# A five-branch mixer: the state-space projections as seven-product jobs, and branch d behind the jobs

## The chip, the cores and the metric

The kernel runs on 1 core of a Trainium2 chip. The metric is the device time of one execution in microseconds (us). A core has five engines that run their own instruction streams in order: TensorE (PE, matmuls), VectorE (DVE), ScalarE (ACT), GpSimd (POOL) and SyncE (SP, which here issues most DMAs). They wait for each other by semaphores.

## What is computed

One layer of a mixer over L = 1024 tokens and 1024 channels: one input projection feeds five branches, each is projected to 1024 channels, and the five are merged by sigmoid gates. The parts of the reference that matter here are branch d and the merge:

```python
def causal_depthwise_conv(x, w, b=None):
    ...
    y = xp[:, 0:L] * w[0]
    for j in range(1, K):            # K = 4
        y = y + xp[:, j:j + L] * w[j]
    return y if b is None else y + b

def ssd_branch(z, xbc, dt_in, conv_w, conv_b, a_log, dt_bias, d_skip, norm_g):
    xbc = jax.nn.silu(causal_depthwise_conv(xbc, conv_w, conv_b))
    xs, bm, cm = split(xbc)          # 512, 2 x 128, 2 x 128 channels
    dt = softplus(dt_in + dt_bias); cs = cumsum(dt * a)      # per chunk of 128 tokens
    xdt = xs * dt
    lmat = where(incl, exp(cs[t] - cs[s]), 0)
    cb = einsum('bncgd,bnsgd->bngcs', cm, bm)
    y_diag = einsum('bngcs,bngrcs,bnsgrp->bncgrp', cb, lmat, xdt)
    states = einsum('bnsgd,bngrs,bnsgrp->bngrpd', bm, decay_states, xdt)
    ...                              # scan over the chunks gives s_prev
    y = y_diag + y_off + xs * d_skip
    return rms_norm(y * silu(z), norm_g)

for p in range(5):
    merged = merged + sigmoid(h @ w_gate[p]) * (ys[p] @ w_branch[p])
x = x + merged @ w_out
```

## The kernel before

**Products.** Every fp32 operand is split into a high and a low part, and a 128x512 product is three matmuls per 128 of K (high by high, high by low, low by high). A *direct* projection of a block of 128 channels over 1024 tokens (`proj_in`, tile `gin`) is 8 K-steps x 2 halves x 3 = 48 matmuls. A gate block (`gate_half`, tile `gate`) is as many.

**Seven-product jobs.** `seven` computes two blocks of 128 channels at once, as a 2x2 block product with seven instead of eight half products: 7 x 12 = 84 matmuls (tile `pm`) instead of 96. The sums of weights it needs (`factors`: `fs`) are made on POOL, their split on ACT (`fh`) and DVE (`fl`), and seven DVE steps (`u`, `c`, `x`) put the products together. The sums of the token operand, which all jobs share, are made once before the first job, in the pool `ct`: 16 POOL sums `r`, DVE sums and splits (`fs`, `s`, `t1l`, `t2l`, `t4l`), at last `h01l`. The products lie in eight PSUM banks (`open_banks("pt", x=8)`, handed out in turn). The results go to DRAM and a branch fetches them with `loaded`.

**Stages**, with their times in the trace: a prologue with the token index scores of branch c (to 175 us); branch a (to 555.6); branch d with its twelve direct blocks, and four gate blocks between its steps (`marks`, `gate_mm`), then `ct`, with c's block `c_k` and the last gate block (to 816.6); 30 jobs, 14 for projections of b, m and c and 16 for gates (to 1390.5); branch b and branch m (to 1559.5); branch c; the output projection. A merge multiplies one branch's result by `w_branch` (16 half blocks of 12 matmuls, tile `proj`, 192 in all), and adds it under its gate. The order of merges is `seq` = (0, 3, 1, 4, 2): branch a, d, b, m, c. Merge 0 is put beside branch b and merge 1 beside m, by `issue_after`: a half block may be issued after a given matmul of the branch, these marks lying `evenly` in it.

**Branch d** works in two groups of four heads. A group takes four blocks (two of `x`, one each of B and C), each a `conv_silu`: three shifted DVE products over 1023, 1022 and 1021 columns, a Tanh and a closing product. Eight units follow, one for 128 tokens, two of them in flight (`skew`): `lm` loaded by a DMA, four DVE steps (subtract, min), Exp on ACT, four DVE products with `dt` and the masked `cb`; then `pyd`, `pyo` and the state `dst`, with four POOL steps (`xw`, `xs`, `ytd`, `dst`). At the end, four blocks `zs` of z and eight gates (`yz`, `yf`).

**Top-k.** The selection of branch c is 192 pairs of DVE steps (MAX8 and MATCH_REPLACE8). `share` tells which part of them is put between the DVE work of branch a, branch d and the stage t (`ct` and the jobs).

Of the kernel before, what the change touches and what calls it, by code (L numbers as in the profile page):

```python
# [55 lines left out]
def mixer_body(ctx, tc, a, out):  # L56
# [1075 lines left out]
    def gate_mm(p, cb, mark, w):
        for hv in HV:
            with tc.issue_after(mark):
                run(gate_half(p, cb, hv, w))

    fill = []
    for (p, cb), mark in zip(units[len(done):], marks):
        fill.append((p, cb, mark, gate_w(p, cb)))
        if len(fill) < len(marks):  # L1140
# [271 lines left out]
```

## Time and profile before

| | us |
|---|---|
| median of 3 runs | 1928.08 (1925.49 to 1933.24) |
| the profiled execution | 1928.29 |
| its span | 1926.6 |
| PE busy | 1819.6 (94%) |
| DVE busy | 1535.1 (80%) |
| ACT busy | 765.1 (40%) |
| POOL busy | 546.0 (28%) |

The span is the time from the first to the last instruction that the hardware profiler recorded. A busy time counts an engine's instructions, overlaps once. The granted clock of PE is 1.0 at its full level, 2.4 GHz, and 0.5 at the lower one, 1.2 GHz. Idle time of an engine is shown before a row in square brackets with what ended it.

### The profile page before, as it was taken

How to read it: one execution, taken by the hardware profiler on the slowest of the kernel's cores; microseconds unless marked ns; L12 is line 12 of the kernel's file. 1: busy time of each engine (PE TensorE's matmuls, PEld its weight loads, DVE VectorE, ACT ScalarE, POOL GpSimd, SP SyncE). 2: the span in 40 equal slices, each digit the busy share in tenths (PEclk: the TensorE clock that was granted, in tenths of full speed). 3: DMA queues.
4: the chain of work that ended last, by engine and by line, in shares of the span. 5: the costliest groups of instructions: out<-in, count | busy, mean ns of one | idle time of the engine just before them, and what ended most of it. 6: DMA issues, size and time to landing. Idle time of an engine off the chain costs nothing.

```text
span 1926.6 us, 30311 instructions
## 1 busy us (share of the span) xinstructions
PE 1819.6 (94%) x11116; PEld 1490.7 (77%) x11116; DVE 1535.1 (80%) x2684; ACT 765.1 (40%) x1455; POOL 546.0 (28%) x518
## 2 busy tenths in 40 slices
PE   6999999999999999699999999999988989999888
PEld 5788787878788777588888888888766668887767
DVE  7679979788757997987787878777777669997874
ACT  6466242424234413333222234333334546764231
POOL 5102212121102232432222222222024254434144
PEclk9999999999999999899999999999999999999999
DMA  6412111111122222133333333332478353224533
GB/s 195 122 50 55 51 39 51 40 45 50 46 72 55 66 50 83 67 120 115 104 115 112 107 115 108 117 110 99 142 234 277 111 170 116 89 88 155 166 114 129
DMA packets 187909, 199.88 MB, mean 104 GB/s; under 512 B 23641, under 2 KB 139214, under 8 KB 187762
## 3 DMA queue, kind: packets, MB, share of 16 engines
q1 hardware_dynamic: 187186, 196.91, 32.5%
q8 instruction: 88, 1.44, 0.3%
q10 hardware_dynamic: 576, 1.05, 0.1%
q14 instruction: 59, 0.48, 0.1%
HBM read 141.67 MB, written 52.05 MB: 101 GB/s over the span
## 4 chain that ended last, share of the span: by engine, by line
PE 71%; DVE 16%; issue 4%; DMA 3%; ACT 3%; POOL 2%; SPq 0%; POOLq 0%; DVEq 0%; ACTq 0%
PE pm L50 31%; PE gin L50 13%; PE proj L50 8%; PE po L50 3%; PE lg L50 2%; PE gate L50 2%; DVE sc L50 2%; PE pT L50 2%; PE ix L50 2%; DVE m L50 1%; DVE cacc L50 1%; PE t L50 1%; PE t2y L50 1%; DVE wlo L50 1%; DVE lm L50 1%
## 5 line engine op out<-in xcount | busy, mean ns | idle before, releaser
L50 PE MATMUL proj<-part,whi 128*128 128x512 f32 x640 | 209.4, 402 | 7.8 <-DVE tgl L50 2.8
L50 DVE MAX8 m<-sc 128x8 f32<-128x384 f32 (+5 forms) x192 | 170.3, 888 | 1.6
L50 DVE MATCH_REPLACE8 sc<-m,sc 128x384 f32<-128x384 f32 (+5 forms) x192 | 168.0, 875 | 0.0
L105 ACT ACTIVATE fh<-fs 128x512 fp32r<-128x512 f32 x132 | 83.1, 632 | 193.7 <-PE pm L50 188.0
L50 PEld LDWEIGHTS proj<-part,whi 128*128 128x128 f32 x640 | 120.6, 191 | 34.4 <-DVE tgl L50 4.0
L50 PE MATMUL proj<-part,wlo 128*128 128x512 f32 x320 | 128.2, 401 | 4.8 <-DVE wlo L50 4.8
L105 ACT ACTIVATE whi<-wraw 128x512 fp32r<-128x512 f32 x106 | 66.3, 629 | 144.0 <-PE gin L50 94.3
L50 DVE SCALAR_TENSOR_TENSOR u<-pm,u 128x512 f32<-128x512 f32 x128 | 85.0, 684 | 47.5 <-PE pm L50 47.2
L105 ACT ACTIVATE fh<-gr 128x512 fp32r<-128x512 f32 x90 | 56.8, 632 | 145.6 <-PE pm L50 113.5
L50 DVE TENSOR_TENSOR fl<-fs,fh 128x512 fp32r<-128x512 f32 x132 | 93.8, 713 | 3.5 <-ACT fh L105 3.5
L1187 POOL TENSOR_TENSOR fs<-gr 128x512 f32<-128x512 f32 x30 | 39.0, 1301 | 184.3 <-DVE fl L50 183.5
L1333 POOL TENSOR_TENSOR mg<-mg,tgl 128x512 f32<-128x512 f32 x48 | 67.8, 1416 | 57.2 <-DVE tgl L50 52.5
L50 DVE TENSOR_TENSOR fl<-gr,fh 128x512 fp32r<-128x512 f32 x90 | 64.1, 713 | 24.5 <-ACT fh L105 24.5
L50 DVE SCALAR_TENSOR_TENSOR cacc<-craw,pc,cacc 128x1023 f32<-128x1023 f32 (+2 forms) x60 | 77.6, 1293 | 3.6 <-ACT cacc L543 3.2
L50 DVE TENSOR_TENSOR wlo<-wraw,whi 128x512 fp32r<-128x512 f32 x82 | 60.2, 738 | 18.7 <-ACT whi L105 13.7
L50 PEld LDWEIGHTS proj<-part,wlo 128*128 128x128 f32 x320 | 60.8, 190 | 16.8 <-DVE wlo L50 5.2
L1186 POOL TENSOR_TENSOR fs<-gr 128x512 f32<-128x512 f32 x30 | 39.4, 1315 | 116.8 <-issue 116.8
L910 ACT ACTIVATE lg<-lg,mx,rq 128x128 f32<-128x128 f32 (+7 forms) x64 | 55.0, 861 | 18.7 <-DVE mx L50 16.4
L50 DVE SCALAR_TENSOR_TENSOR lg<-sc,cf,lg 128x384 f32<-128x384 f32 (+3 forms) x96 | 56.2, 604 | 6.8 <-POOL cf L889 3.8
L50 PE MATMUL pm<-h00h,fl 128*128 128x512 f32 x120 | 47.8, 398 | 12.6 <-DVE fl L50 12.6
L50 DVE SCALAR_TENSOR_TENSOR sc<-rl,iwt,sc 128x512 f32<-128x512 f32 (+3 forms) x84 | 47.0, 615 | 12.2 <-ACT rl L463 11.0
L922 ACT ACTIVATE pt<-pT 128x512 f32<-128x512 f32 (+3 forms) x96 | 43.1, 484 | 34.1 <-PE po L50 25.9
(601 smaller groups left out, 5628.1 us busy)
## 6 DMA issues: line engine op xcount, KB each, us to landing
tgl<-gd SPq DMA_DIRECT2D x80, 256.0 KB, 2.8
wraw<-in_w_in_dram SPq DMA_DIRECT2D x66, 256.0 KB, 2.8
gr<-in_w_gate_dram SPq DMA_DIRECT2D x32, 512.0 KB, 3.6
gr<-in_w_in_dram SPq DMA_DIRECT2D x28, 512.0 KB, 3.7
yr<-yd SPq DMA_DIRECT2D x40, 256.0 KB, 4.0
wraw<-in_w_branch_dram SPq DMA_DIRECT2D x40, 256.0 KB, 3.5
yd<-sg SPq DMA_DIRECT2D x16, 512.0 KB, 3.4
gd<-u SPq DMA_DIRECT2D x30, 256.0 KB, 4.0
```

The costliest lines, as they stand in the source:

```text
L50: r = f(*args, **kw)
L105: S.activation(hi, raw, AF.Copy)
L910: S.activation(lg[:, :W], lg[:, :W], AF.Exp, scale=rq[:, 2 * j + hf:2 * j + hf + 1], bias=mx[:, hf:hf + 1], accum_out=sm[:, hf:hf + 1])
L922: S.activation(pt[:, i0 * P:(i0 + n) * P], ps[:, :n * P], AF.Copy)
L1186: eng.tensor_tensor(s3, a11, a21, OP.subtract)
L1187: eng.tensor_tensor(s1, a21, a22, OP.add)
L1333: (G if n < 4 else V).tensor_tensor(m, m, t, OP.add)
```

## The change

- The eight blocks of `d_xbc` and the four of `d_z` are no longer direct blocks of branch d. They become six seven-product jobs: four for `d_xbc`, in the fifth to eighth place of the list, and two for `d_z` behind `c_gate`.
- The four jobs of `d_xbc` have the convolution as an epilogue, `conv_halves`: it works on the halves of 512 tokens as they leave `seven`, with its sums in PSUM banks from the same eight (`cacc`, two for each block), and small extra products where the second half needs the last tokens of the first.
- Branch d comes behind all jobs and loads its blocks. Merge 0 is now beside it; merge 1 is beside b and m together.
- The four gate blocks that stood between the steps of d are now made one after the other behind `c_k`.
- `share` gives branch a 0.25 and the stage t 0.75 of the top-k steps, d none.
- In a unit of d the four subtract-and-min steps become four ACT Relu, `dt` is put on `xs` instead of `lm` (a POOL product `xd` more; `xw` is made from it), and the four products with `cbm` become one DVE product of 512 columns.

```diff
@@ z blocks through DRAM
+          (..., ("d_z", 4), ("d_xbc", 8))}
@@ branch_d
-                tl.append(conv_silu(gp, proj_in(OFF["d_xbc"] + blk * P), [scw[:, j, blk:blk + 1] for j in range(4)],
-                                    ssdb[:, blk:blk + 1], "dc", "dc", 4))
+                tl.append(loaded(gp, "d_xbc", blk, "dc", 6))
...
                 for r in range(4):
-                    V.tensor_scalar(lm[:, r, :], lm[:, r, :], cs[:, n, 8 + 4 * g + r:9 + 4 * g + r], 0.0, OP.subtract, OP.min)
-                S.activation(flat(lm), flat(lm), AF.Exp)
-                for r in range(4):
-                    V.scalar_tensor_tensor(lm[:, r, :], lm[:, r, :], dtt[:, n, 4 * g + r:4 * g + r + 1], cbm, OP.mult, OP.mult)
+                    S.activation(lm[:, r, :], lm[:, r, :], AF.Relu, scale=-1.0, bias=cs[:, n, 8 + 4 * g + r:9 + 4 * g + r])
+                S.activation(flat(lm), flat(lm), AF.Exp, scale=-1.0)
+                V.tensor_tensor(lm, lm, cbm[:, None, :].to_broadcast([P, 4, P]), OP.mult)
                 xsn = v4(xs[:, n, :])
+                xd = gp.tile([P, 4, 64], F32, name="xd", tag="xd", bufs=2)
                 xw = gp.tile([P, 4, 64], F32, name="xw", tag="xw", bufs=2)
-                G.tensor_tensor(xw, xsn, b3(dte[:, n, hs], 4, 64), OP.mult)
+                G.tensor_tensor(xd, xsn, b3(dtt[:, n, hs], 4, 64), OP.mult)
+                G.tensor_tensor(xw, xd, b3(eds[:, n, hs], 4, 64), OP.mult)
...
-        zs = [silu2(gp, proj_in(OFF["d_z"] + b * P), "zs", "dc", 4) for b in range(4)]
+        zs = [silu2(gp, halves(loaded(gp, "d_z", b, "zr", 1)), "zs", "dc", 6) for b in range(4)]
...
-    share = {"a": 0.3, "d": 0.1, "t": 0.6}
+    share = {"a": 0.25, "t": 0.75}
...
     branch("a", branch_a)
-    branch("d", branch_d)
...
-        gate_mm(*fill[-1])
+        for _ in gate_steps(4):
+            pass
...
+    def conv_halves(c, cw, cb):
+
+        acc = [bank("cacc") for _ in c]
+        for y, x in zip(acc, c):
+            S.activation(y, x, AF.Identity, scale=cw[3], bias=cb)
+        for j in (2, 1, 0):
+            d = 3 - j
+            for y, x in zip(acc, c):
+                V.scalar_tensor_tensor(y[:, d:], x[:, :512 - d], cw[j], y[:, d:], OP.mult, OP.add)
+            V.scalar_tensor_tensor(acc[1][:, :d], c[0][:, 512 - d:], cw[j], acc[1][:, :d], OP.mult, OP.add)
+        for y, x in zip(acc, c):
+            S.activation(x, y, AF.Tanh)
+            V.scalar_tensor_tensor(x, x, 1.0, y, OP.add, OP.mult)
...
+            cs4 = seven(ga, w, mov)
+            if f == "conv":
+                for i in range(2):
+                    conv_halves(cs4[2 * i:2 * i + 2], [scw[:, j, b + i:b + i + 1] for j in range(4)], ssdb[:, b + i:b + i + 1])
...
     next(first)
+    branch("d", branch_d)
+    m0 += evenly(span["d"], 16)
+    run(first)
+    m0 = []
+    first = merge_steps(1, m0)
+    next(first)
...
     branch("b", branch_b)
-    m0 += evenly(span["b"], 16)
-    run(first)
     branch("m", branch_m)
     kmx.close()
-    merge(1, [None] * 4 + evenly(span["m"], 12))
+    m0 += evenly(span["b"] + span["m"], 16)
+    run(first)
```

Three places in the order of instructions. On DVE, where the sums of the job operands begin, before (`flo` is the low part of a gate block's weights, `fs`, `s`, `r`, `t1l`, `t2l`, `t4l` are the sums, `yz`, `yf` the gates of branch d):

```order
L50 TENSOR_SCALAR dss<-dss 128x1
L50 TENSOR_TENSOR yf<-pyT,pc 128x512
L50 TENSOR_SCALAR yz<-yz,dss 128x512
L50 MATCH_REPLACE sc_128<-m_68,sc_128 128x768
L50 TENSOR_TENSOR yf<-pyT,pc 128x512
L50 TENSOR_TENSOR flo<-fraw,fhi 128x512
L50 TENSOR_TENSOR fs<-r_7526,r_7528 128x512
L50 TENSOR_TENSOR flo<-fraw,fhi 128x512
L50 TENSOR_TENSOR s_7524<-r_7530,r_7526 128x512
L50 TENSOR_TENSOR fs<-r_7530,fs 128x512
L50 TENSOR_TENSOR t1l<-fs,t1h 128x512
L50 TENSOR_TENSOR r_7532<-fs,r_7532 128x512
```

The end of the same sums after the change:

```order
L50 TENSOR_TENSOR t4l<-r_5726,t4h 128x512
L50 TENSOR_TENSOR s_5679<-r_5744,r_5740 128x512
L50 TENSOR_TENSOR fs<-r_5744,fs 128x512
L50 TENSOR_TENSOR t1l<-fs,t1h 128x512
L50 TENSOR_TENSOR r_5746<-fs,r_5746 128x512
L50 TENSOR_TENSOR t2l<-fs,t2h 128x512
L50 TENSOR_TENSOR flo<-fraw,fhi 128x512
L50 TENSOR_TENSOR t4l<-r_5746,t4h 128x512
L50 TENSOR_TENSOR flo<-fraw,fhi 128x512
L50 MAX m_68<-sc_129 128x8
L50 MATCH_REPLACE sc_129<-m_68,sc_129 128x640
L50 MAX m_69<-sc_129 128x8
```

Before, the low parts of the gate blocks stand among the last gates of branch d and at the head of the sums; after, the second block's stands behind all sums, with the top-k steps behind it.

On DVE inside a job of `d_xbc`, after (before there is no such job; `x`, `u` and `c` are the four half blocks, `pc` the convolution's weights):

```order
L50 SCALAR_TENSOR_TENSOR cacc<-c_6864,pc,cacc 128x510
L50 SCALAR_TENSOR_TENSOR cacc<-u_6859,pc,cacc 128x509
L50 SCALAR_TENSOR_TENSOR cacc<-u_6862,pc,cacc 128x510
L50 SCALAR_TENSOR_TENSOR cacc<-x,pc,cacc 128x3
L50 SCALAR_TENSOR_TENSOR cacc<-c_6864,pc,cacc 128x2
L50 SCALAR_TENSOR_TENSOR cacc<-c_6864,pc,cacc 128x509
L50 SCALAR_TENSOR_TENSOR cacc<-u_6862,pc,cacc 128x509
L50 SCALAR_TENSOR_TENSOR x<-x,cacc 128x512
L50 SCALAR_TENSOR_TENSOR u_6859<-u_6859,cacc 128x512
L50 SCALAR_TENSOR_TENSOR cacc<-c_6864,pc,cacc 128x3
L50 SCALAR_TENSOR_TENSOR u_7040<-pm,x 128x512
L50 TENSOR_TENSOR fl<-fs,fh 128x512
```

Rows of the epilogue follow each other; those of `seven` (`u<-pm`) and of the next factors (`fl`) stand between, and nearly no top-k.

On PE between the last mixing of branch b (`mix`) and the first transposes of branch m (`pqm`), before, where 123 `proj` matmuls stand between the two; these are the last rows:

```order
L50 MATMUL proj<-part,wlo 128x512
L50 MATMUL proj<-part,whi 128x512 x2
L50 MATMUL pqm<-ident,qm 128x128 x8
L50 MATMUL lgm<-kTm,qm 128x256 x4
L50 MATMUL proj<-part,wlo 128x512
L50 MATMUL proj<-part,whi 128x512
L50 MATMUL pqm<-ident,qm 128x128 x8
L50 MATMUL lgm<-kTm,qm 128x256 x4
```

After the change 24 `proj` matmuls stand between them, of which the last rows are these:

```order
L50 MATMUL proj<-part,whi 128x512 x2
L50 MATMUL proj<-part,wlo 128x512
L50 MATMUL pqm<-ident,qm 128x128 x8
L50 MATMUL lgm<-kTm,qm 128x256 x4
L50 MATMUL pqm<-ident,qm 128x128 x8
L50 MATMUL lgm<-kTm,qm 128x256 x4
L50 MATMUL proj<-part,whi 128x512 x2
```

The merge that filled this place is now beside branch d, and the next one's 16 half blocks are spread over b and m.

## Rows read from the trace of the kernel before

**Rows 1.** the page: the span, then busy time of each engine, its share and instructions
```profile
span 1926.6 us, 30311 instructions
PE 1819.6 (94%) x11116; PEld 1490.7 (77%) x11116; DVE 1535.1 (80%) x2684; ACT 765.1 (40%) x1455; POOL 546.0 (28%) x518
```

**Rows 2.** stretches: their us, then PE, PEld, DVE, ACT, POOL busy, PEclk, DMA
```profile
555.60:816.60 261.00, 234.96 (x1153) 192.72 (x1151) 230.13 (x419) 88.22 (x154) 80.45 (x90) 0.98 0.24 67
816.60:1390.50 573.90, 573.16 (x2519) 474.32 (x2520) 447.26 (x687) 194.32 (x314) 152.24 (x117) 1.00 0.34 112
1390.50:1559.50 169.00, 150.13 (x719) 116.49 (x718) 122.37 (x232) 74.82 (x166) 60.89 (x48) 0.98 0.62 208
1443.50:1478.00 34.50, 28.91 (x127) 23.06 (x126) 25.05 (x31) 10.98 (x19) 17.80 (x14) 0.99 0.86 288
1478.00:1532.30 54.30, 50.42 (x233) 36.44 (x233) 42.40 (x103) 37.49 (x99) 15.92 (x12) 0.97 0.41 144
```

**Rows 3.** the same for one group of branch d, then its gates
```profile
609.00:638.00 29.00, 25.87 (x147) 21.56 (x146) 28.61 (x78) 6.68 (x11) 16.33 (x26) 1.00 0.24 60
740.00:764.00 24.00, 21.62 (x122) 16.94 (x121) 20.32 (x41) 8.91 (x22) 8.58 (x11) 1.00 0.43 132
```

**Rows 4.** timeline of the SP queue and of PE, from b to m
```profile
1442.68 0.34 SPq L846 DMA_DIRECT2D yd<-sg  x1
...
1452.95 0.32 SPq L846 DMA_DIRECT2D yd<-sg  x1
...
1460.49 0.32 SPq L846 DMA_DIRECT2D yd<-sg  x1
...
1469.20 0.32 SPq L846 DMA_DIRECT2D yd<-sg  x1
...
1471.44 0.59 SPq L531 DMA_DIRECT2D qm<-z_m_q  x1
...
1477.84 1.94 PE L50 MATMUL pqm<-ident,qm 128*128 128x128 f32 x8 [4.51 <-DMA qm<-z_m_q]
```

**Rows 5.** timeline (start, us): DVE and POOL while the sums of job operands run
```profile
766.33 0.68 DVE L50 TENSOR_TENSOR fs<-r,r 128x512 f32<-128x512 f32 x1
...
770.05 1.77 DVE L50 TENSOR_TENSOR t1l<-fs,t1h 128x512 fp32r<-128x512 f32 x1
...
773.45 0.68 DVE L50 TENSOR_TENSOR t2l<-fs,t2h 128x512 fp32r<-128x512 f32 x1
...
798.04 0.67 DVE L50 TENSOR_TENSOR t4l<-r,t4h 128x512 fp32r<-128x512 f32 x1
...
769.61 1.67 POOL L1164 TENSOR_TENSOR r<-h01h,h01l 128x512 f32<-128x512 f32 x1 [1.23 <-DVE s L50]
```

**Rows 6.** groups of the page: xcount, busy us, mean ns, idle before
```profile
L50 DVE MAX8 m<-sc 128x8 f32<-128x384 f32 (+5 forms) x192 | 170.3, 888 | 1.6
...
L50 DVE MATCH_REPLACE8 sc<-m,sc 128x384 f32<-128x384 f32 (+5 forms) x192 | 168.0, 875 | 0.0
...
L50 DVE SCALAR_TENSOR_TENSOR cacc<-craw,pc,cacc 128x1023 f32<-128x1023 f32 (+2 forms) x60 | 77.6, 1293 | 3.6 <-ACT cacc L543 3.2
```

**Rows 7.** stretches around the first job, columns as in rows 2
```profile
804.00:812.00 8.00, 0.70 (x2) 0.26 (x2) 7.86 (x12) 3.23 (x6) 4.46 (x4) 0.57 0.28 93
...
816.00:820.00 4.00, 2.66 (x6) 2.15 (x7) 4.00 (x5) 0.00 (x0) 1.60 (x1) 0.50 0.38 115
...
820.00:824.00 4.00, 4.00 (x14) 3.15 (x13) 3.06 (x4) 1.12 (x2) 3.07 (x2) 0.73 0.49 147
```

**Rows 8.** groups of POOL in branch d
```profile
L1000 POOL TENSOR_TENSOR ytd<-ytd,xs 128x256 f32<-128x256 f32 x16 | 13.8, 864 | 4.7 <-DVE ytd L50 4.7
...
L989 POOL TENSOR_TENSOR xw<-xs,dte 128x256 f32<-128x256 f32 x16 | 12.8, 807 | 85.0 <-ACT xs L964 85.0
...
L994 POOL TENSOR_TENSOR xs<-xs,dskip 128x256 f32<-128x256 f32 x16 | 11.3, 703 | 23.4 <-PE pyd L50 19.6 <-DVE cbm L50 3.7
...
L1005 POOL TENSOR_TENSOR dst<-dst,cdd 128x256 f32<-128x256 f32 x14 | 9.2, 655 | 8.1 <-DVE dst L50 6.2 <-DVE ytd L50 1.8
```

More of the change, by code (lines that the diff above doesn't have):

```diff
@@ L173, in mixer_body @@
     bte = keep.tile([P, NT, 4], F32, name="bte")
-    dte = keep.tile([P, NT, 8], F32, name="dte")
+    pad = keep.tile([P, NT, 8], F32, name="pad")
     ecs = keep.tile([P, NT, 8], F32, name="ecs")
@@ L188, in mixer_body @@
     zd = {nm: dp.tile([n, P, L], F32, name="z_" + nm) for nm, n in
-          (("b_u", 4), ("b_v", 4), ("b_gate", 4), ("m_q", 4), ("m_gate", 4), ("c_q", 4), ("c_gate", 4), ("c_k", 1))}
+          (("b_u", 4), ("b_v", 4), ("b_gate", 4), ("m_q", 4), ("m_gate", 4), ("c_q", 4), ("c_gate", 4), ("c_k", 1), ("d_z", 4), ("d_xbc", 8))}
     ctx.enter_context(tc.tile_pool(name="edge", bufs=1, side="right")).tile([P, 40], F32, name="edge")
@@ L992, in unit @@
                 for r in range(4):
-                    T.matmul(pyd[:, r * 64:(r + 1) * 64], lm[:, r, :], xsn[:, r, :], start=True, stop=True)
+                    T.matmul(pyd[:, r * 64:(r + 1) * 64], lm[:, r, :], xd[:, r, :], start=True, stop=True)
                 G.tensor_tensor(xsn, xsn, b3(dskip[:, hs], 4, 64), OP.mult)
@@ L1127, in mixer_body @@
     branch("a", branch_a)
-    branch("d", branch_d)
-    marks = evenly(span["d"], 4)
     units = units[:len(done) + 4]
[L1132 to L1140, printed above, removed]
-            gate_mm(*fill[-1])
     v0 = len(V.log)
@@ L1227, in seven @@
         return c11, c12, c21, c22
+    def conv_halves(c, cw, cb):
[10 more added lines that the diff above has]
+            V.scalar_tensor_tensor(x, x, 1.0, y, OP.add, OP.mult)
     seq = (0, 3, 1, 4, 2)
     jobs = [(w_in[:, OFF[nm] + b * P:OFF[nm] + (b + 2) * P], zd[nm], b, f, 1.0)
-            for nm, f in (("b_v", AF.Gelu_apprx_tanh), ("b_u", AF.Gelu_apprx_tanh), ("b_gate", None),
-                          ("m_q", None), ("m_gate", None), ("c_q", None), ("c_gate", None)) for b in (0, 2)]
+            for nm, f in (("b_v", AF.Gelu_apprx_tanh), ("b_u", AF.Gelu_apprx_tanh), ("d_xbc", "conv"), ("b_gate", None),
+                          ("m_q", None), ("m_gate", None), ("c_q", None), ("c_gate", None),
+                          ("d_z", None)) for b in range(0, zd[nm].shape[0], 2)]
     jobs += [(a["w_gate"][0, p, :, cb * P:(cb + 2) * P], gd[p], cb, AF.Tanh, 0.5) for p in seq for cb in range(0, KT, 2) if (p, cb) not in units]
@@ L1244, in mixer_body @@
                         r[0][:, :, :P], r[1][:, :, :P], r[0][:, :, P:], r[1][:, :, P:])
-            for i, c in enumerate(seven(ga, w, mov)):
-                if f:
+            cs4 = seven(ga, w, mov)
+            if f == "conv":
+                for i in range(2):
+                    conv_halves(cs4[2 * i:2 * i + 2], [scw[:, j, b + i:b + i + 1] for j in range(4)], ssdb[:, b + i:b + i + 1])
+            for i, c in enumerate(cs4):
+                if f and f != "conv":
                     S.activation(c, c, f, scale=scale)
```

4 lines of the change are left out of this document (1 added, 3 removed).

## The prediction

> **What bounds the kernel now.** The first view is the page's busy line: TensorE (PE) works 1819.6 of 1926.6 us, so only 107.0 us of the span are not matmul time [rows 1]. A change gains here by taking matmuls away, and loses by opening new holes; the question is which weighs more. The second view is the stretches [rows 2]. From 816.6 to 1390.5 us the thirty seven-product jobs run: PE 573.2 of 573.9 us, DVE 447.3. That stage is PE at its pace, 573.9 / 2519 = 0.228 us a matmul and 573.9 / 30 = 19.13 us a job. From 555.6 to 816.6 branch d, the c_k projection and four gate blocks run: PE 235.0 of 261.0, so 26 us of holes. From 1390.5 to 1559.5 branches b and m run with merges 0 and 1 between: PE 150.1 of 169.0, so 19 us of holes. The third view is how the chains look inside these two: in one group of branch d DVE is busy 28.6 of 29.0 us while PE is not full [rows 3], and between b's last mixing and m's first transposes PE ends with 4.5 us idle for a DMA [rows 4]. So branches d, b and m are chains of small steps; projections and merge products fill them.
>
> **What is removed and added on PE.** Branch d's twelve direct blocks take 12 x 48 = 576 matmuls; as six jobs they take 6 x 84 = 504. The 72 fewer are worth 72 x 0.228 = 16.4 us. That is the whole gain, and it is certain. Everything else is placement: 576 matmuls, 131 us, leave the stretch in which they filled branch d's chain, and 115 us of jobs go to a stage that has no hole to fill. I write the sum by stretches.
>
> **Before the jobs (261.0 us now).** What is left there is c_k and four gate blocks: 48 + 192 = 240 matmuls, 54.7 us. It can't go at that pace, because DVE has more to do. Counted from the order of the changed kernel: 27 sums for the job operands now stand in one piece ahead of the second gate block's last split. In the trace this piece runs from 766.3 to about 797.9, 31 us [rows 5]. Behind it stand six weight splits at 0.68 (4 us), 22 top-k steps at 0.88 (19 us; means in [rows 6]) and four last splits (2.5 us), then the first job's factor: 31 + 4 + 19 + 2.5 = 57. Before, the same pieces left PE without work from about 804 to 816.6, and at half clock (0.57, and 0.73 after it) [rows 7]. I take 65: DVE's 57, some waiting of one engine for the other, and the first matmuls at half clock. Bounds are 56 (PE never waits) and 72 (as much idle as today). Term: 65 - 261 = **-196**.
>
> **The jobs.** Six more at 19.13 are **+114.8**. Whether DVE keeps up is the second question. Top-k costs 170.3 + 168.0 = 338.3 us of DVE [rows 6], 0.6 of it now in this stage: 203. The rest of the 447.3 is 244, or 8.1 a job. A job with convolution adds 12 half-row products and 4 closing ones. The full-row product takes 1.29 [rows 6], so a half about 0.64: 16 x 0.64 = 10.2, and some tiny rows at the seam, 0.5. That makes 8.1 + 10.7 = 18.8 without any top-k, and top-k almost stops there by the order (three rows in four jobs). So those four are even with PE. The share of top-k in this stage rises to 0.75, 254 us, and what the convolution jobs push back stands in the ten jobs after them, 11 to 13 rows a job by the order: 8.1 + 9.7 to 11.4 = 17.8 to 19.5 against 19.13. DVE passes PE here and there by a microsecond or less; factors are kept about one job ahead, which absorbs some. The epilogue holds four of the eight PSUM banks of the next job's products until it ends, some 12 us after the job; the next job wants the first of them after four of its seven products, 11 us in. I take **+6** for all of it, between 0 (all absorbed) and 24 (each of 15 jobs late by 1.6).
>
> **Branch d beside merge 0.** Now it is a chain of its own with only 192 merge products (43.7 us) between. Its own small matmuls took 235.0 - 816 x 0.228 = 49 us in the old stretch (816 = 576 + 240), so PE's floor is 93. A unit is lighter on DVE: of eight 128x128 steps four become one product of 512 columns, and four go to ACT. It is heavier on POOL, one more product: 2 x 0.807 + 0.703 + 0.864 + 0.655 = 3.84 us a unit by the means of [rows 8]. The old group ran 8 units in 29 us, 3.6 each [rows 3]. 16 units at 3.84 are 61; each of the two groups has a start (a block from DRAM, four-block transposes with ACT copies, the first unit's chain) that I estimate at 12 and 8 us; the eight gates took 24 us with twice the PE work and I keep 22; 52 merge products stand behind them in a row, 11.8. Sum: 61 + 20 + 22 + 12 = **+115**. Bounds: 95 (PE's floor) and 127 (units at 4.6, as if the old DVE pace came on top of POOL's).
>
> **Branches b and m beside merge 1 alone (169.0 us now).** 192 merge products, 43.7 us, leave; 19 us of holes are there already. By the order 63 instead of 101 stand before b's last mixing, 24 instead of 123 between it and m's first transposes, 78 behind m. Up to the mixing I take 44 instead of 53 (38 x 0.228 = 8.7 less). The stretch behind it lasts 34.3 us now, with 28.9 of PE work [rows 2, 4]; with 24 products it is bare, 5.5 us of work. What sets its length is b's four output blocks: they go to DRAM at 1442.7, 1453.0, 1460.5 and 1469.2, and m's loads are queued on SP right behind the last, at 1471.4, landing 6.4 us later [rows 4]. That chain doesn't shrink by taking matmuls away, save where it competes with the merge's transfers; I take 28, bounds 20 and 34.5. Then m, 54.3 now at 50.4 of PE, 52, and the tail 78 x 0.228 = 17.8. Sum 44 + 28 + 52 + 18 = 142, term **-27**, bounds 130 and 150.
>
> **Small terms.** Top-k's share beside branch a falls by 0.05 x 338.3 = 17 us of DVE, of which I give PE **-2** (0 to -5). Each new idle stretch brings half clock for a few microseconds, as at 816 to 824 [rows 7]: **+2** (0 to 5). Merges 2 to 4, branch c and the output projection are untouched.
>
> **Sum.** 1926.6 - 196 + 114.8 + 6 + 115 - 27 - 2 + 2 = 1939.4 of span. The profiled run was 1928.29, 1.7 above its span, and 0.2 above the median 1928.08, so no correction is needed: **1941 us**, 0.7% slower. Read as holes: 16.4 us of matmul go, and about 29 us of idle come, 107 to 136.
>
> **Rivals.** (1) *The cover is enough*, faster. With eight DVE steps of a unit turned into one, it goes at 3.1 us, since POOL's means above were taken beside a DVE that was full (in the group of [rows 3] POOL worked only 16.3 us for 8 units, 2.0 each). Then d is 12 shorter, b's chain to m 8 shorter (20, as transfers have less beside them), the jobs' start 7 shorter, and DVE never late, 6: 1941 - 33 = **1908**. It decides at a unit pace of 3.3 us together with a stretch before m of 24. For it: POOL's 2.0; against it: recurrence and gates are latency, which no engine's busy time shows. (2) *Even*: units at 3.2 (-10) and the jobs only 2 late (-4): **1927**. (3) *The epilogue binds*: DVE falls behind in the convolution jobs and the product banks are not free, PE stops four times by about 3 us and in the jobs with the pushed-back top-k by 1: 24 instead of 6, **1959**. It decides where DVE's work in a job passes 19.13 by more than the one job kept ahead. (4) *POOL's extra product slows DVE*: in [rows 5] the same subtraction takes 0.68 us alone and 1.77 while a POOL sum runs. Sixteen more POOL products in d, each stretching one DVE step by 1.09 us on the chain, are +17: **1958**.
>
> The Trainium skill, "Perfetto Trace Analysis", Optimizing Scalar/DVE Operations, says that GpSimd and VectorE share a read port, so that moving work between the two may not help; [rows 5] agree. By that rule (4) is what would happen; by the rows of the old group, where 26 POOL rows ran beside a full DVE at 3.6 us a unit, the price is already in the pace that I use.
>
> **How the numbers follow.** Forecast 0.36, (1) 0.17, (2) 0.27, (3) 0.12, (4) 0.08. A measurement here can tell about 0.5% from no change, 9.6 us: faster is under 1918.4, slower over 1937.7. The forecast's own spread, 1932 to 1952, gives 0.06 of its 0.36 to the middle: faster 0.17, same 0.33, slower 0.50. The forecast, (2) and half of each outer case lie between 1907 and 1960, which leaves out under 0.2.
>
> **What would show it.** In the changed profile: PE busy near 1803 of a span near 1939. Jobs of 19.1 us with at most 0.5 more in the convolution ones and those behind: if they run at 20.5, (3). Units of d at 3.8 us or so from their last products: at 3.1, (1). PE idle 20 us or more in d's stretch and a bare stretch of about 28 before m. If the start of the jobs lies 65 us behind the end of branch a, that term holds. The forecast is wrong where merge 0's products alone keep PE full in d, or where DVE, not POOL, sets the unit.

## The result, and the profile after

The changed kernel takes 1958.5 us (median of 4 runs, 1954.9 to 1962.5), the kernel before 1930.7 in the runs beside it: the ratio is 1.0148, 95% interval 1.0115 to 1.0181. It is slower by 28 us. The forecast was 1941, slower by 0.7%. The profiled execution is the shortest of the four, 3.6 us below the median.

The page after: the span, the busy line, and the granted clock in 40 slices.

```profile
span 1953.2 us, 30409 instructions
...
PE 1815.3 (93%) x11044; PEld 1486.3 (76%) x11044; DVE 1555.4 (80%) x2687; ACT 788.2 (40%) x1535; POOL 596.6 (31%) x558
...
PEclk9999999999998999999999999998987989999999
```

Beside [rows 1], PE works 4.3 us less, not 16.4, and the span is 26.6 longer. So idle grew from 107.0 to 137.9 us, and of the 16.4 us of matmuls that went some 12 came back as slower matmuls: the row of clocks has 7 to 9 where branches d, b and m run.

The stretches after, as in [rows 2] (us, then PE, PEld, DVE, ACT, POOL busy, PEclk, DMA share, GB/s): before the jobs, the 36 jobs, branch d, b to its last mixing, from there to m's first transposes, m, the tail behind m, and the rest.

```profile
553.00:617.50 64.50, 56.98 (x238) 45.83 (x236) 53.28 (x73) 18.98 (x32) 21.09 (x13) 0.92 0.19 66
617.50:1310.20 692.70, 688.82 (x3024) 569.09 (x3025) 601.58 (x948) 241.96 (x401) 189.28 (x145) 1.00 0.35 113
1310.20:1431.90 121.70, 100.47 (x525) 82.20 (x523) 81.80 (x157) 62.41 (x144) 67.23 (x91) 0.92 0.62 180
1431.90:1485.40 53.50, 37.48 (x203) 30.78 (x204) 35.81 (x64) 11.10 (x22) 23.07 (x22) 0.84 0.51 177
1485.40:1515.80 30.40, 5.40 (x24) 4.15 (x23) 11.59 (x15) 4.60 (x8) 12.74 (x9) 0.63 0.69 224
1515.80:1567.30 51.50, 49.31 (x224) 35.47 (x225) 38.69 (x102) 35.67 (x97) 10.59 (x7) 0.95 0.32 111
1567.30:1584.70 17.40, 17.40 (x78) 14.36 (x77) 13.80 (x16) 7.48 (x12) 9.44 (x7) 1.00 0.64 201
1584.70:1953.20 368.50, 340.71 (x2129) 277.84 (x2127) 288.30 (x521) 171.54 (x350) 147.99 (x159) 0.97 0.39 125
```

Read against the forecast's terms:

| stretch | forecast, us | measured, us | off by |
|---|---|---|---|
| branch a's end (before: 555.6) | 553.6 | 553.0 | -0.6 |
| before the jobs | 65 | 64.5 | -0.5 |
| 36 jobs (688.7 + 6) | 694.7 | 692.7 | -2.0 |
| branch d | 115 | 121.7 | **+6.7** |
| b to its last mixing | 44 | 53.5 | **+9.5** |
| to m's first transposes | 28 | 30.4 | +2.4 |
| m and its tail | 70 | 68.9 | -1.1 |
| the rest | 367.1 | 368.5 | +1.4 |
| clock, as a term of its own | 2 | in the rows | -2 |

The sum of the last column, 13.8 us, is what the span is longer than forecast (1953.2 against 1939.4); against the median the forecast is 17.5 short. The stage of the jobs, where the change saves, came out as it should; branch d and b up to its mixing, which lost cover, cost more.

The parts of branch d after (its start, first group, second start, second group, gates, and the merge products behind them):

```profile
1310.20:1330.40 20.20, 10.12 (x53) 7.09 (x51) 10.34 (x16) 13.15 (x27) 4.36 (x6) 0.90 0.82 260
1330.40:1361.00 30.60, 27.34 (x143) 23.72 (x144) 20.06 (x43) 17.16 (x46) 22.84 (x34) 0.84 0.59 156
1361.00:1369.40 8.40, 4.84 (x22) 3.70 (x22) 2.93 (x6) 6.02 (x15) 3.64 (x5) 0.87 0.47 159
1369.40:1396.50 27.10, 24.97 (x137) 21.42 (x136) 21.12 (x42) 13.44 (x33) 24.09 (x34) 0.91 0.37 111
1396.50:1420.00 23.50, 21.66 (x123) 17.08 (x122) 20.33 (x43) 7.58 (x19) 8.87 (x12) 1.00 0.65 189
1420.00:1431.90 11.90, 11.53 (x51) 9.20 (x49) 7.01 (x11) 5.06 (x8) 3.43 (x3) 1.00 0.94 255
```

The units and gates are near the forecast (57.7 us for two groups, where 61 were put, 23.5 for the gates, where 22 were put). The first start is 20.2 us and not 12. From one execution to another d varies by some 4 us: it takes 124.4 us in the trace of e6 and 125.8 in that of e3 (both below), which change nothing in it.

### The profile page after: what moved, and what is told of

Same layout as the page of the kernel before. It is cut to its first block, busy times and chain, and to the rows that moved or that the text cites. A ratio compares the mean times of both kernels' runs of the same rounds, so it can differ in the third digit from the quotient of the medians.

```text
span 1953.2 us, 30409 instructions
## 1 busy us (share of the span) xinstructions
PE 1815.3 (93%) x11044; PEld 1486.3 (76%) x11044; DVE 1555.4 (80%) x2687; ACT 788.2 (40%) x1535; POOL 596.6 (31%) x558
## 5 line engine op out<-in xcount | busy, mean ns | idle before, releaser
L50 DVE MAX8 m<-sc 128x8 f32<-128x896 f32 (+5 forms) x192 | 170.4, 888 | 2.1
L50 DVE MATCH_REPLACE8 sc<-m,sc 128x896 f32<-128x896 f32 (+5 forms) x192 | 168.2, 876 | 0.0
L50 DVE SCALAR_TENSOR_TENSOR u<-pm,u 128x512 f32<-128x512 f32 x152 | 100.6, 681 | 30.5 <-PE pm L50 30.1
L50 DVE TENSOR_TENSOR fl<-fs,fh 128x512 fp32r<-128x512 f32 x156 | 112.4, 724 | 11.0 <-ACT fh L105 10.8
L1175 POOL TENSOR_TENSOR fs<-gr 128x512 f32<-128x512 f32 x36 | 47.5, 1321 | 207.1 <-DVE fl L50 202.7
L1174 POOL TENSOR_TENSOR fs<-gr 128x512 f32<-128x512 f32 x36 | 47.5, 1321 | 179.3 <-issue 104.3
L50 DVE TENSOR_TENSOR fl<-gr,fh 128x512 fp32r<-128x512 f32 x108 | 81.0, 753 | 20.0 <-ACT fh L105 20.0
L1340 POOL TENSOR_TENSOR mg<-mg,tgl 128x512 f32<-128x512 f32 x48 | 68.5, 1430 | 74.8 <-DVE tgl L50 64.5
L105 ACT ACTIVATE whi<-wraw 128x512 fp32r<-128x512 f32 x82 | 51.3, 628 | 97.2 <-PE gin L50 58.2
L1177 POOL TENSOR_TENSOR fs<-gr,fs 128x512 f32<-128x512 f32 x36 | 47.1, 1310 | 71.0 <-DVE fl L50 70.8
L1176 POOL TENSOR_TENSOR fs<-fs,gr 128x512 f32<-128x512 f32 x36 | 47.4, 1317 | 44.8 <-DVE fl L50 44.5
L50 PE MATMUL pm<-t2h,fh 128*128 128x512 f32 x144 | 57.1, 397 | 3.9 <-ACT fh L105 3.9
L50 DVE SCALAR_TENSOR_TENSOR sc<-rl,iwt,sc 128x512 f32<-128x512 f32 (+3 forms) x84 | 47.1, 616 | 13.1 <-ACT rl L462 11.9
```

Of the source, the lines that this page charges most:

```text
L50: r = f(*args, **kw)
L105: S.activation(hi, raw, AF.Copy)
L1174: eng.tensor_tensor(s3, a11, a21, OP.subtract)
L1175: eng.tensor_tensor(s1, a21, a22, OP.add)
L1176: eng.tensor_tensor(s2, s1, a11, OP.subtract)
L1177: eng.tensor_tensor(s4, a12, s2, OP.subtract)
```

## Experiments

Ratios are to the kernel before in the runs of the same chip. The theory to test (A): the loss is the chains of branches d, b and m, which stand bare now that d's projections are in the jobs. Against it: (B) the loss is DVE work pushed into the stage of the jobs, and (C) it is the extra POOL product of a unit.

**e1_conv_in_d: is it the epilogue?** The jobs of d_xbc without epilogue, the convolution in branch d.

```diff
-                tl.append(loaded(gp, "d_xbc", blk, "dc", 6))
+                raw = loaded(gp, "d_xbc", blk, "craw", 1)
+                acc = gp.tile([P, L], F32, name="cacc", tag="cacc", bufs=2)
+                S.activation(acc, raw, AF.Identity, scale=scw[:, 3, blk:blk + 1], bias=ssdb[:, blk:blk + 1])
+                for j in (2, 1, 0):
+                    d = 3 - j
+                    V.scalar_tensor_tensor(acc[:, d:], raw[:, :L - d], scw[:, j, blk:blk + 1], acc[:, d:], OP.mult, OP.add)
+                t = gp.tile([P, L], F32, name="dc", tag="dc", bufs=4)
+                S.activation(t, acc, AF.Tanh)
+                V.scalar_tensor_tensor(t, t, 1.0, acc, OP.add, OP.mult)
+                tl.append(t)
...
-        zs = [silu2(gp, halves(loaded(gp, "d_z", b, "zr", 1)), "zs", "dc", 6) for b in range(4)]
+        zs = [silu2(gp, halves(loaded(gp, "d_z", b, "craw", 1)), "zs", "dc", 4) for b in range(4)]
...
-            for nm, f in (("b_v", AF.Gelu_apprx_tanh), ("b_u", AF.Gelu_apprx_tanh), ("d_xbc", "conv"), ("b_gate", None),
+            for nm, f in (("b_v", AF.Gelu_apprx_tanh), ("b_u", AF.Gelu_apprx_tanh), ("d_xbc", None), ("b_gate", None),
```

> The changed kernel, but the four jobs of d_xbc have no epilogue: branch d loads the raw blocks and makes the convolution itself, as before the change. Theory A (the loss is that branches d, b and m stand bare: their chains lost the matmuls that covered them): eight blocks of 3 x 1.29 + 1.22 us on DVE and 2 x 1.06 on ACT come on d's chain, d grows from 121.7 us by 25 to 40, the jobs get 4 shorter: 1980 to 1995 us. Theory B (the loss is DVE work pushed into the stage of the jobs, the epilogue above all): the jobs get shorter by 10 or more and d has room: 1950 or less.

Measured: 2005.3 us, 1.0384 (1.0363 to 1.0405). The jobs, then branch d:

```profile
617.80:1305.20 687.40, 686.27 (x3024) 567.25 (x3024) 548.91 (x854) 225.82 (x368) 188.54 (x145) 1.00 0.35 113
1305.20:1480.80 175.60, 107.52 (x527) 87.92 (x525) 122.01 (x190) 81.37 (x163) 76.04 (x93) 0.80 0.46 137
```

The jobs end 5 us earlier than with the epilogue (687.4 against 692.7), and d is 54 longer. Made beside the jobs instead of in d, the epilogue saves 47 us: 53 us more of DVE work lengthen the jobs by only 5. Not all of the 47 is the convolution itself, since the raw blocks and z come through one buffer in e1, and ACT waits 17 us for the loads into it. Theory B, that DVE work pushed into the jobs is the loss, falls for the epilogue.

**e3_share_b: is it top-k?**

```diff
-    share = {"a": 0.25, "t": 0.75}
+    share = {"a": 0.25, "t": 0.6, "b": 0.15}
```

> The changed kernel with the stage of the jobs at its old share of top-k steps, 0.60 instead of 0.75, and the other 0.15 (51 us of DVE) beside branch b. It prices what the pushed top-k costs. Theory A: the jobs take 692.7 us where 36 at 19.04 are 685.5, so at most 7 us come back; b, with DVE at 36 of 53.5 us, loses 3 to 10 on its chain: 1953 to 1962 us. Theory B (DVE in the stage of the jobs is the loss): 1945 or less.

Measured: 1965.4 us, 1.0170 (1.0140 to 1.0201). The jobs, and m:

```profile
617.70:1311.40 693.70, 688.63 (x3024) 568.50 (x3025) 561.41 (x887) 243.30 (x401) 189.37 (x145) 1.00 0.35 113
1526.00:1584.80 58.80, 56.27 (x250) 41.76 (x251) 57.50 (x129) 37.49 (x100) 13.98 (x9) 0.93 0.32 111
```

With 40 us less of DVE work the jobs take 693.7 us, as long as before (692.7): the 0.75 costs nothing there, and with that theory B falls for top-k too. Beside b and m it costs: m takes 58.8 and not 51.5.

**e2_old_unit and e4_before_unit: the unit.** The old unit in the changed kernel (e2), and the new unit in the kernel before (e4), which is the same edit in the other direction.

```diff
-                    S.activation(lm[:, r, :], lm[:, r, :], AF.Relu, scale=-1.0, bias=cs[...])
-                S.activation(flat(lm), flat(lm), AF.Exp, scale=-1.0)
-                V.tensor_tensor(lm, lm, cbm[:, None, :].to_broadcast([P, 4, P]), OP.mult)
+                    V.tensor_scalar(lm[:, r, :], lm[:, r, :], cs[...], 0.0, OP.subtract, OP.min)
+                S.activation(flat(lm), flat(lm), AF.Exp)
+                for r in range(4):
+                    V.scalar_tensor_tensor(lm[:, r, :], lm[:, r, :], dtt[...], cbm, OP.mult, OP.mult)
...
-                G.tensor_tensor(xd, xsn, b3(dtt[:, n, hs], 4, 64), OP.mult)
-                G.tensor_tensor(xw, xd, b3(eds[:, n, hs], 4, 64), OP.mult)
+                G.tensor_tensor(xw, xsn, b3(pad[:, n, hs], 4, 64), OP.mult)
```

> The changed kernel with the old unit in branch d: eight DVE steps of 128 columns instead of four ACT Relu and one DVE product, one POOL product less. Theory A: the unit is a bare chain now, seven more DVE rows of 0.28 to 0.34 us lengthen it by 0.5 to 1 us a unit: 1966 to 1975 us. Rival C (the extra POOL product, and what it does to DVE, made d longer than forecast): 16 x 1.09 us less: about 1942.

> The kernel before with the new unit in branch d alone. In the kernel before DVE is busy 28.6 of 29.0 us in a group while PE is not full, so taking seven DVE rows from each unit should shorten both groups. Theory A: 3 to 5 us a group: 1921 to 1925 us. If POOL sets the unit (rival C): no gain or a loss, 1930 to 1937.

Measured: e2 1980.9 us, 1.0258 (1.0233 to 1.0283), 22 us more than the changed kernel; e4 1925.7 us, 0.9969 (0.9956 to 0.9982). In e2 the units of branch d with their second start, then the gates:

```profile
1332.50:1407.50 75.00, 59.50 (x268) 51.20 (x269) 61.42 (x179) 15.25 (x27) 35.49 (x57) 0.73 0.32 82
1407.50:1439.00 31.50, 27.92 (x138) 21.90 (x138) 22.50 (x43) 9.48 (x22) 8.71 (x11) 0.93 0.64 200
```

Branch d takes 146.9 us instead of 121.7. The units take 75.0 (66.1 with the new unit), with DVE busy 61.4 of them and PE 59.5, so no engine is full and it is a chain; the gates behind take 31.5 (23.5), and more products stand behind these. Why the gates are longer too wasn't taken apart. The new unit is worth 22 us where d stands bare. In the kernel before it is worth little: 0.3% in e4, and two more kernels with it, e8 and e11 below, show none. Rival C, the extra POOL product, isn't the loss: with it the units take 57.7 us, less than the 61 of the forecast, which had it in. Its own price wasn't taken apart from the gain on DVE, and it needn't be nothing: in the second group POOL works 24.1 of 27.1 us. The Trainium skill, "Perfetto Trace Analysis", Optimizing Scalar/DVE Operations, says that where these engines aren't saturated but hold up others, breaking up instructions may complete work sooner. No run here tests that by itself: e2 breaks the DVE product of 512 columns into four of 128, but it also brings four steps from ACT to DVE and drops a POOL product, and its units take 9 us more.

**e5_d_bare: how long is d by itself?** Nothing beside d, merge 0 beside b and merge 1 beside m, as in the kernel before.

```diff
-    m0 += evenly(span["d"], 16)
-    run(first)
-    m0 = []
-    first = merge_steps(1, m0)
-    next(first)
...
+    m0 += evenly(span["b"], 16)
+    run(first)
...
-    m0 += evenly(span["b"] + span["m"], 16)
-    run(first)
+    merge(1, [None] * 4 + evenly(span["m"], 12))
```

> The changed kernel with the merges where they were before the change: merge 0 beside branch b, merge 1 beside branch m, and nothing beside branch d. It shows how long d's chain is by itself. Theory A (chains, each needing cover): d takes 95 to 110 us instead of 121.7, since only the 52 merge products behind its gates and a few on the chain go; b and m come back to about 169 from 152.9: 1955 to 1965 us in all, so that the place of the merge matters little and the 192 products are only moved from one bare chain to another. Rival D (merge 0's transfers and products are what slows d): d falls to 90 or less and the sum to 1945.

Measured: 1957.3 us, 1.0131 (1.0107 to 1.0154), as long as the changed kernel. Branch d, b to its mixing, and to m's first transposes:

```profile
1309.50:1428.50 119.00, 66.24 (x334) 57.58 (x332) 66.41 (x133) 54.47 (x131) 60.33 (x87) 0.71 0.47 138
1428.50:1475.30 46.80, 43.65 (x244) 35.77 (x245) 33.77 (x65) 10.90 (x22) 14.95 (x16) 0.94 0.55 189
1475.30:1505.80 30.50, 27.93 (x123) 22.75 (x122) 24.51 (x31) 10.94 (x18) 14.92 (x10) 1.00 0.87 300
```

The first row carries the case. Without a single merge product the stretch of branch d takes 119.0 us, with merge 0 beside it 121.7. The ends of the two differ. In e5 PE waits for branch b's first operand, `wsr`, whose load stands on SP behind d's outputs:

```profile
1428.48 1.11 PE L50 MATMUL wsT<-ident,wsr 128*128 128x128 f32 x4 [6.62 <-POOL wsr L813]
```

In the changed kernel the 11.9 us of products behind the gates stand there, and the wait is 0.4 us. Without these ends d takes 112.4 us bare (119.0 - 6.6) and 109.8 with products beside it (121.7 - 11.9), which is the same within the 4 us by which traces of d differ. So its length is its own, and the 141 products beside it, 32 us of matmuls, were free. But the same products were as useful beside b and m, since the whole kernel takes as long. The clock, a mean over times at its full and its half level, shows what a bare chain does besides: 0.71 over d, and PE busy 66.2 us for d's own matmuls, where the prediction got 49 from [rows 2], in a stretch that was covered.

**e9_merge_d_b: do the products decide?**

```diff
-    m0 += evenly(span["d"], 16)
-    run(first)
-    m0 = []
-    first = merge_steps(1, m0)
-    next(first)
...
-    m0 += evenly(span["b"] + span["m"], 16)
+    m0 += evenly(span["d"] + span["b"], 16)
+    run(first)
+    branch("m", branch_m)
...
+    merge(1, [None] * 4 + evenly(span["m"], 12))
```

> The changed kernel with merge 0 spread over d and b together and merge 1 beside m, as before the change. By the order 60 merge products leave the end of d, where they stood in a row with no chain beside them; 60 instead of 24 stand between b's mixing and m, 114 instead of 78 behind m. Theory A: d 13.6 shorter, b to its mixing unchanged at 53, the stretch behind it unchanged at 30 (its length is not PE's), 8 more behind m: 1952 to 1955 us. If PE's work set these stretches, the products would only move: 1958.

Measured: 1959.8 us, 1.0139 (1.0111 to 1.0166), no gain. Branch d, the stretch before m, the tail behind m, and what PE waits for at the end of d:

```profile
1311.30:1429.10 117.80, 85.98 (x466) 71.34 (x464) 73.86 (x146) 56.64 (x135) 63.64 (x89) 0.90 0.60 175
1480.00:1510.30 30.30, 13.85 (x60) 10.82 (x59) 19.51 (x22) 6.29 (x11) 15.20 (x10) 0.80 0.75 260
1565.80:1590.50 24.70, 24.70 (x110) 20.41 (x109) 12.57 (x17) 7.36 (x12) 14.66 (x11) 1.00 0.63 191
...
1429.08 1.11 PE L50 MATMUL wsT<-ident,wsr 128*128 128x128 f32 x4 [7.89 <-POOL wsr L813]
```

The stretch before m is 30.3 us with 60 products, 30.4 with 24 (the changed kernel) and 30.5 with 123 (e5). So PE doesn't set its length, as I had said. But of the 13.6 us of products that left the end of d, d gave back only 3.9: without them PE waits 7.9 us for `wsr` there, as in e5. The tail behind m grew by 7.3. The expectation missed by taking every product off as a gain.

**e6_ring and e8_before_unit_ring: what sets the stretch before m.** Branch b's gates and outputs in the four buffers that are free once vg is read.

```diff
-            sg = silu2(gp, halves(loaded(gp, "b_gate", g, "gr", 1)), "sg", None, 1)
+            sg = silu2(gp, halves(loaded(gp, "b_gate", g, "vg", 4)), "sg", "vg", 4)
```

> The changed kernel with branch b's gates and outputs (gr, sg) in the four buffers that vg leaves free, instead of one buffer each. Between b's mixing and m's first transposes PE works 5.4 of 30.4 us, and each Tanh of a gate waits for the output of the one before to be written. Theory A: this stretch gets 10 to 14 us shorter and nothing else moves: 1944 to 1949 us. Theory B: no change, 1958.

Measured: 1950.0 us, 1.0098 (1.0077 to 1.0120), 8.5 us less than the changed kernel. The changed kernel first, the last of the four output writes in the SP queue with m's load behind it, then ACT and PE; what ended a wait stands in brackets:

```profile
1510.94 0.32 SPq L845 DMA_DIRECT2D yd<-sg  x1
1511.37 0.37 SPq L530 DMA_DIRECT2D qm<-z_m_q  x1
...
1499.29 1.15 ACT L523 ACTIVATE sg<-gr 128x512 f32<-128x512 f32 x2 [8.00 <-DMA yd<-sg]
...
1507.64 1.15 ACT L523 ACTIVATE sg<-gr 128x512 f32<-128x512 f32 x2 [7.20 <-DMA yd<-sg]
...
1515.81 1.52 PE L50 MATMUL pqm<-ident,qm 128*128 128x128 f32 x6 [25.01 <-DMA qm<-z_m_q]
```

These Tanh of a gate waited 7 to 8 us for the DMA that writes the output before it (one buffer), and m's loads stand behind the last of these on SP, as in [rows 4]. The same stretch in e6:

```profile
1488.40:1510.20 21.80, 5.40 (x24) 4.14 (x23) 11.19 (x10) 2.42 (x4) 12.42 (x8) 0.69 0.70 237
```

21.8 us instead of 30.4. So the single buffers of b's gates and outputs cost 8.6 us of it; the edit lengthens both rings, and the waits above name the outputs' one. What sets the 21.8 stays open. In the kernel before I expected 3 to 5 us from the same edit:

> The kernel before with two things that were found useful: the new unit of branch d (it alone gave 1925.7 against 1931.6) and the four buffers for branch b's gates and outputs. Before, the stretch from b's mixing to m's first transposes was covered by merge products but for 4.5 us of idle. Theory A: 3 to 5 us from the ring on top of the 6 from the unit: 1920 to 1923 us. If the two stand in each other's way: 1926.

Measured: 1930.0 us, 0.9993 (0.9977 to 1.0008): nothing. The stretch before m and the tail behind m in e8, then in e4, which lacks the longer ring:

```profile
1440.20:1467.70 27.50, 24.71 (x103) 20.04 (x102) 19.19 (x24) 5.47 (x9) 12.56 (x8) 0.94 0.78 266
1524.00:1558.60 34.60, 34.60 (x155) 28.57 (x154) 17.14 (x21) 8.63 (x14) 21.67 (x17) 1.00 0.61 186
```

```profile
1441.20:1473.00 31.80, 28.13 (x123) 22.60 (x122) 24.27 (x31) 11.41 (x19) 17.76 (x12) 1.00 0.89 301
1529.70:1556.80 27.10, 26.90 (x119) 21.86 (x118) 13.11 (x18) 7.36 (x12) 14.84 (x11) 1.00 0.61 185
```

4.3 us of the stretch went and 7.5 came on in the tail: where products cover the chain, a shorter chain only leaves them for later.

**e14_lm4, e10_d_loads_first, e15_rings: branch d's own chain.** e14 gives `lm` four buffers instead of three.

```diff
-                lm = gp.tile([P, 4, P], F32, name="lm", tag="lm", bufs=3)
+                lm = gp.tile([P, 4, P], F32, name="lm", tag="lm", bufs=4)
...
-            yz = gp.tile([P, BW], F32, name="yz", tag="lm", bufs=3)
+            yz = gp.tile([P, BW], F32, name="yz", tag="lm", bufs=4)
```

> The changed kernel with four instead of three buffers for the tile lm (and the gates that use its place) in branch d. In the trace of the changed kernel ACT waits for the DMA into lm again and again: a load takes 5.8 us to land, and with Relu, Exp, the product and pyd behind it a buffer is busy for some 11.5 us, which with three buffers is 3.9 us a unit. Theory E (the ring of lm sets the unit): four buffers let a unit go at 3.2 us or so, d gets 8 to 12 shorter: 1947 to 1951 us. The forecast's reason (POOL's five products of a unit, 3.84 us): no change, 1958.

Measured: 1957.3 us, 1.0134 (1.0113 to 1.0155), no gain that can be told. What PE, ACT and the others waited for in the changed kernel's `lm`, the landing time of its loads, then the same wait in e14:

```profile
  DMA lm<-csd: 17.6, 9
...
DMA to landing us min/median/max: 4.6/5.8/6.5
```

```profile
  DMA lm<-csd: 6.1, 5
```

And d in e14 to the last unit, then its gates:

```profile
1309.20:1387.60 78.40, 60.77 (x330) 50.14 (x329) 48.67 (x98) 47.10 (x113) 54.74 (x76) 0.89 0.56 163
1387.60:1419.20 31.60, 27.79 (x150) 22.04 (x149) 25.22 (x49) 10.37 (x24) 9.45 (x12) 1.00 0.63 191
```

The waits for lm fell from 17.6 to 6.1 us, and the last unit came 78.4 us after d's start, 8 earlier than in the changed kernel (86.3). From one unit's pyd to the next it is 3.8 us in the first group and 3.7 in the second, in e14 3.4 and 3.5, which makes about half of the 8 us; the other half lies between the groups. So the ring of `lm` held the units of the changed kernel. In the second group POOL stands close behind it, and with four buffers it is full there:

```profile
1361.80:1387.60 25.80, 22.82 (x132) 18.32 (x132) 19.94 (x42) 13.91 (x35) 25.57 (x35) 1.00 0.40 113
```

That is 3.2 us of POOL a unit. My 3.84 us, put on POOL, came out near the truth by luck: POOL's products take less, and the loads of `lm` made up for it. But the gates then waited for the z blocks, which come through one buffer (ACT waited 4.7 and 6.4 us for two of these loads): they took 31.6 us and ended where they had before.

e10 issues d's first loads ahead of most of merge 0's operand.

```diff
+    branch("d", branch_d)
...
-    branch("d", branch_d)
```

> The changed kernel with the loads of branch d's first group issued ahead of five of the eight loads of merge 0's operand, which stand between them on the SP queue now. The first 20.2 us of d have PE busy 10.1; I had put 12 on this head. If the queue is the reason: the head gets 4 to 7 shorter, 1951 to 1955 us. If the head is the chain of transposes, Relu, Exp and product: 1958, or more where merge 0 then comes late.

Measured: 1956.0 us, 1.0136 (1.0121 to 1.0152). Its start, and the products behind the gates:

```profile
1310.20:1320.50 10.30, 7.98 (x48) 6.20 (x45) 4.99 (x9) 9.78 (x21) 3.48 (x6) 1.00 0.71 225
1406.00:1427.30 21.30, 21.30 (x95) 17.56 (x94) 10.36 (x16) 5.89 (x10) 4.53 (x4) 1.00 0.92 297
```

In the changed kernel the last two of d's first four blocks stand on SP behind three loads (`yr`) of merge 0, and the first units' `lm` behind two more:

```profile
1298.72 3.87 SPq L530 DMA_DIRECT2D dc<-z_d_xbc  x2
1312.36 1.63 SPq L1319 DMA_DIRECT2D yr<-yd  x3
1314.04 0.90 SPq L530 DMA_DIRECT2D dc<-z_d_xbc  x2
...
1318.65 1.87 SPq L975 DMA_DIRECT2D lm<-csd  x3
...
1330.45 1.94 PE L50 MATMUL pyd<-xd,lm 128*128 128x64 f32 x8 [6.21 <-DVE lm L50]
```

That is the 20.2 us: with the order turned the start takes 10.3. Again the products came out behind, 21.3 us instead of 11.9, and the kernel gains 2.6 at the medians, which is within the noise.

e15 has the rings of e6 and e14, and z loaded into the ring of `dc`.

```diff
-                tl.append(loaded(gp, "d_xbc", blk, "dc", 6))
+                tl.append(loaded(gp, "d_xbc", blk, "dc", 7))
...
-        zs = [silu2(gp, halves(loaded(gp, "d_z", b, "zr", 1)), "zs", "dc", 6) for b in range(4)]
+        zs = [silu2(gp, halves(loaded(gp, "d_z", b, "dc", 7)), "zs", "dc", 7) for b in range(4)]
```

> The changed kernel with three rings made longer: four buffers for lm, b's gates and outputs in the four that vg leaves (both as tried alone: no gain that can be told, and 8.5 us), and the z blocks loaded into the ring of dc, now seven deep, instead of one buffer of their own (with lm longer, the gates of d waited 11 us for the z blocks, which came one after another). Theory A: units at 3.3 us, gates straight behind them, the stretch before m at 22; but by the order only 93 instead of 123 merge products then stand between the steps of d, the other 99 behind them, so d gives back 7 of some 15 us: 1940 to 1945 us. If the rings were the whole loss: 1930 or less.

Measured: 1950.8 us, 1.0107 (1.0085 to 1.0129), as e6 alone. d to the last unit, and the products behind its gates:

```profile
1315.60:1392.60 77.00, 58.65 (x311) 49.33 (x309) 47.80 (x94) 47.27 (x114) 54.16 (x76) 0.87 0.55 166
1418.00:1436.80 18.80, 18.80 (x84) 15.49 (x83) 10.10 (x15) 4.85 (x9) 3.23 (x3) 1.00 0.89 277
```

The profiled execution is the longest of the five, 1957.4. The chain is 9 us shorter, 77.0, and 7 of them stand behind it as products, 18.8 instead of 11.9. PE had room for these products: it was idle 18.4 of the 77.0 us. It is the order on PE that puts them behind the gates, and they end some 7.5 us after `wsr` is there. An order that keeps them between the units wasn't tried.

**e11_before_unit_share: the kernel before with the new unit and the new shares.**

```diff
-    share = {"a": 0.3, "d": 0.1, "t": 0.6}
+    share = {"a": 0.25, "t": 0.75}
```

> The kernel before with the new unit and the changed shares of top-k (0.25 beside a, 0.75 beside the jobs, none beside d). The share of 0.75 cost the jobs nothing that could be seen (1309.9 against 1311.2 us for their end at 0.60), and branch d was DVE-bound in the kernel before. Expected: the 6 us of the unit (1925.7) and 3 to 7 more, 1918 to 1923 us. If d is not held by DVE any more once the unit is light: 1926.

Measured: 1929.9 us, 0.9999 (0.9988 to 1.0010), no gain. Branch a ends 4 us earlier than in e4 and d's gates 5 us (754 against 759), d itself is as long (199.6 against 200.5), and the first job starts at 802 in both, waits some 11.5 us for a split on DVE behind its first two matmuls, and goes on at 814. What was won in front went into the stretch before the jobs, where DVE has the pushed top-k steps and is busy 46.8 of 47.9 us. No version beat both kernels by more than the 0.3% of e4.

## Why the prediction was right or wrong

- **Direction and reason: right.** 72 matmuls less, and more idle than that: the forecast had 29 us of idle more, 31 came. PE is now idle 21 of the 121.7 us of branch d, 16 of 53.5 to b's mixing and 25 of 30.4 before m, which 16.4 us of matmuls can't pay for. e5 shows that d's length is its own. e2 and e6 show that a heavier unit and a shorter wait in a bare chain move the total, by 22 and 8.5 us, where the same edits in the kernel before give 6 us (the unit, e4) and nothing (both, e8).
- **Size: too small**, 0.7% for 1.5%. 1958.5 us lies above the forecast's own spread, 1932 to 1952, and next to the numbers of rivals (3) and (4), but the rows speak against the reasons of both (below).
- **The clock: +2 was put, some 12 came.** PE is busy 1815.3 us and not 1803, while the idle time is nearly as forecast, so that by the busy line slower matmuls are most of the 13.8 us. How much of this lengthens a chain isn't shown: d alone takes 112.4 us at a clock of 0.71 (e5) and 109.8 at 0.91.
- **Before the jobs: right**, 64.5 for 65, and by the step that was named. PE waits there for the splits that stand behind the sums (idle in brackets):

```profile
580.21 0.79 PE L50 MATMUL gate<-h10h,fhi 128*128 128x512 f32 x1 [3.39 <-ACT fhi L105]
...
584.32 0.80 PE L50 MATMUL gate<-h10h,flo 128*128 128x512 f32 x1 [2.89 <-DVE flo L50]
```

- **The jobs: right**, 692.7 for 694.7. PE is idle 3.9 us in the whole stage. e3 shows that top-k's part of it is nothing, and e1 that the epilogue's is 5 us.
- **Branch d: 6.7 us too short**, by one part, which is 8.2 short, "each of the two groups has a start that I estimate at 12 and 8 us". The first took 20.2: I didn't count the loads of merge 0's operand on the SP queue ahead of d's blocks (e10). The 61 for the units is near (57.7), in part by luck (e14): POOL's five products take 2.9 to 3.2 us a unit and not 3.84, in keeping with rival (1)'s doubt about means that were taken beside a full DVE, and the ring of `lm` held the unit at 3.7 to 3.8 all the same.
- **b to its mixing: 9.5 too short**, the largest miss of a stretch, and the step that failed is "44 instead of 53 (38 x 0.228 = 8.7 less)". I took PE's work off a stretch that I had called a chain. It takes 53.5 with 63 products, and took 53 with 101, in the kernel before:

```profile
1390.50:1443.80 53.30, 43.90 (x245) 35.01 (x244) 41.68 (x80) 19.25 (x37) 12.26 (x14) 0.97 0.69 229
```

  PE's idle time there went from 9.4 to 16.0 us. In e5, with 101 products, it takes 46.8 and in e9 50.9; both have the operand of the running merge loaded and split earlier, beside d. What of that is the operand's work on DVE and ACT and what the clock (0.84, and 0.94 in e5) wasn't taken apart.
- **The stretch before m: nearly right**, 30.4 for 28. 8.6 us of it are b's single buffers (e6); I had only named the queue behind them.
- **The rivals.** (1) and (2) needed units of 3.1 or 3.2 us; e14 and e15 came part of the way (3.4 to 3.6) and gained nothing in d, since the gates wait for z (e14) or the order puts more products behind them (e15). As far as the units got shorter, that alone didn't give their time, and POOL, full at 3.2 us a unit in the second group of e14, leaves hardly more to win. (3) falls: it needs 18 us more in the jobs, 712.7, and they take 692.7; e1 and e3 say the same. (4) wasn't tested alone, but it needs 17 us more in the units, and they take 57.7 instead of 61; the one DVE product of a unit takes 0.68 us at the shortest and 0.92 in the median, so 0.24 more and not 1.09.

## What to carry to other kernels

A matmul that covers a chain of small steps costs little (141 products beside branch d added nothing to it that can be told), so making it cheaper saves little: count a saving on PE only against the idle that its absence leaves, and price a bare chain by its own waits, with no share of PE's work taken off. Before shortening a part of a chain, ask what then stands behind it: rings made longer in branch d and an earlier start came back as products behind it, which the order on PE put there, and of these edits only the one in the stretch before m, where PE had nothing else to do, came out in the total. In a bare chain look first at the rings of one to three buffers and at what stands ahead of its loads on the queue.
